# Moving six gathers of a side stream behind the third head of an attention stage, and loading a unit's queries in one transfer

## The chip, the cores and the metric

One core of one Trainium2 chip runs the whole program. The metric is device time in microseconds (us) per execution. The program is written in Tile, where the author gives the order of the work by tracing it, and a planner then places each instruction on its engine's queue by its own estimate of when its operands are ready; an engine then runs its queue strictly in that order.

## The reference

One step of a one-layer decoder over a new prompt of 2048 tokens and over eight running sequences with 8 new tokens each, all in float32:

```python
fq, fk, fv, flogf, mq, mk, mv, ig, lf, og, conv_new = _mixer_inputs(xp, ...)   # one input projection
fox_h = _fox_prompt(fq, fk, fv, flogf)      # 8 heads of 64: causal attention with a forget bias
(C_p, n_p, m_p), m_h = _mlstm_prompt(...)   # 4 heads of 128: matrix memory by chunks
xp = _block_out(xp, fox_h, m_h, ...)        # w_o, layer norm, squared-ReLU MLP 1024-4096-1024, layer norm
k_past = cache_k[l][page_table]             # the sample: 8 sequences with 8192 paged past keys and values
sfox_h = _fox_sample(sq, sk, sv, slogf, k_past, v_past, logf_past)
xs = _block_out(xs, sfox_h, sm_h, ...)
```

## The kernel before

The main line has four stages. Stage A projects the inputs (with the matrix memory beside it). Stage B (`phase_b`) is the prompt's attention. Stage O (`phase_o`) multiplies by `w_o` and norms. Stage C (`phase_c`) is the MLP in four blocks of tokens (`ci` 0 to 3), each with 16 slices of the hidden width (`fc` 0 to 15). Nearly all products are written as three matmuls on float32 split in a high and a low part (`mm3`, lines 157 to 159).

**The stream.** The sample's attention runs beside the main line as a Python generator, `sample_attention`. Each `yield` ends a step. `tick(us)`, which the main line calls with its own estimate of the work just traced, calls `attend()` once per `acc[2]` microseconds, and `attend()` traces the next step; in stages O and C that is every 5 us. A step turns keys, multiplies them (`qk_step`), multiplies values (`pv_step`) and issues the gathers of later pages. `k_gather` (line 1545) is an indirect DMA of 128 rows of 4 KB, 512 KB, issued by POOL into the ring `kT`; `v_gather` (line 1662) does the same for values. `beside` ties every instruction of a step behind the last instruction of the main line on its engine, as far as the dictionary `last` names one.

In stage A the ring has four places. Behind step 78 (`NA + 2`) the stream yields 3, which parks it. The second ring, six places in memory that stage A used, exists from stage B on: the stream then does six gathers of its own with a yield after each of the first five, and goes on with step 79 in the sixth round:

```python
        if n == NA + 2:
            yield 3
            for i in range(6):
                k_gather(NA + i)
                if i < 5:
                    yield 1
```

In stage B `acc[2]` is infinite, so `tick` traces no step there. The loop over units calls `attend()` by hand for units 10 to 15.

At `fc == 13` of block `ci == 2` the main line calls `tick(100.0)` until the stream has ended, and then `sampled()`: the stream's last instructions reduce to `mixs` (line 1706), SP writes that to `dmix` (line 1782), and `sampled` reads `dmix` back as `mxs` (line 1294), splits it into `mhs` and `mls`, and multiplies it by `w_o`.

**Stage B.** 64 units: 8 heads `h`, 8 groups `g` of 256 queries, in that order. `queries(z, g)` (line 970) loads a unit's 64 x 256 queries twice, into partitions 0 to 63 and 64 to 127 of `qn` (three buffers), then ACT splits off `qh` and DVE `ql`. `keys` loads 512 keys of a head, POOL doubles them (`dup`, line 939), PE turns them, ACT and DVE split them into `ks`. `scores(z, g)` works on two tiles of 128 queries: POOL adds the diagonal mask (`nd`, line 990, three buffers), PE multiplies (lines 997 and 998), DVE adds the forget values and takes the maximum (lines 1004 and 1008). `values` of a unit runs one unit later. In head 0 the keys and forget values (`nl`, line 945; `vn`, line 946) come in four parts; those of a later head are loaded during the head before. All of these loads are issued by SP, whose queue also holds the four loads of `w_o` for stage O.

Of the kernel before, what the change touches and what calls it, by code (L numbers as in the profile page):

```python
# [14 lines left out]
OP = mybir.AluOpType  # L15
# [10 lines left out]
S = 2048  # L26
# [21 lines left out]
def dap(ap, off, dims):  # L48
    return bass.AP(tensor=ap.tensor, offset=ap.offset + off, ap=[list(d) for d in dims])
# [3 lines left out]
def body(ctx, tc, I, O, stages):  # L53
    nc = tc.nc
    V, A, G, T, SY = nc.vector, nc.scalar, nc.gpsimd, nc.tensor, nc.sync
# [5 lines left out]
    dq = drm.tile([4, 128, S], F32, name="dq")  # L61
# [39 lines left out]
    acc = [0.0, None, PACE_A, None]  # L101
    macc = [0.0, [], PACE_M]
    last = {}
# [10 lines left out]
    def beside(gen):  # L114

        with ExitStack() as es:
            for i in last.values():
                es.enter_context(tc.issue_after(i.ins))
            return next(gen, 0)

    def attend():

        r = beside(acc[1])
        if r == 3:
            acc[3] = acc[1]
        if r in (0, 3):
            acc[1] = None

    def tick(us):

        macc[0] += us
        while macc[1] and macc[0] > macc[2]:
            macc[0] -= macc[2]
            if beside(macc[1][0]) == 0:
                macc[1].pop(0)
        if not macc[1]:
            macc[0] = 0.0
        acc[0] += us
        while acc[1] is not None and acc[0] > acc[2]:
            acc[0] -= acc[2]  # L140
            attend()
# [6 lines left out]
    def split_hi(dst, src, scale=1.0):  # L148
        last["ACT"] = A.activation(dst, src, AF.Copy, scale=scale)  # L149

    def split_lo(dst, src, hi, eng=None):
        r = (eng or V).tensor_tensor(dst, src, hi.bitcast(F32), op=OP.subtract)  # L152
        if eng is None:
            last["DVE"] = r
# [731 lines left out]
    for bi in range(4):  # L886
        g = block_a(bi)
# [21 lines left out]
    def phase_b():  # L909
# [8 lines left out]
        def bank():  # L918

            turn[0] += 1  # L920
            if turn[0] % 3 == 0:
                return pps.tile([128, 512], F32, name="pS", tag="sX", bufs=1)
            return ppb.tile([128, 512], F32, name="pS", bufs=2)

        def head(h):
            vn = Z[0]["vn"] if h == 0 else pb.tile([128, 16, 64], F32, name="vn", bufs=2)
            nl = pb.tile([128, 2048], F32, name="nl", bufs=2)
            if h == 0:
                masks.append(pb.tile([128, 128], F32, name="dmask"))
            ls = pb.tile([128, 32], F32, name="ls", bufs=2)  # L930
            ks = pb.tile([128, 2048], F32R, name="ks", bufs=2)
            G.memset(ls, 1.0)
            return dict(h=h, ls=ls, nl=nl, vn=vn, ks=ks)
# [8 lines left out]
        def forget_values(z, a, n):  # L942

            h = z["h"]
            SY.dma_start(z["nl"][:, a:a + n], dap(dnl, h * TOT + a, [[0, 128], [1, n]]))
            SY.dma_start(z["vn"][:, a // 128:(a + n) // 128], vp[a:a + n, h * 64:h * 64 + 64].rearrange("(t p) c -> p t c", p=128))
# [4 lines left out]
        def keys(z, g, kn=None):  # L951

            h = z["h"]
            kn = keys_load(h, g) if kn is None else kn
            if h == 0:
                forget_values(z, g * 512, 512)
            pt = ppb.tile([128, 4, 128], F32, name="pt", bufs=3)
            for i in range(4):
                T.transpose(pt[:, i], kn[:, i].rearrange("p d c -> p (d c)"), ident)
            pf = pt.rearrange("p i c -> p (i c)")  # L960
            k = z["ks"][:, g * 512:(g + 1) * 512]
            split_hi(k, pf)
            split_lo(k[64:128], pf[64:128], k[64:128])

        def queries(z, g):

            h = z["h"]
            qn = pb.tile([128, 256], F32, name="qn", bufs=3)
            for d in range(2):
                SY.dma_start(qn[d * 64:d * 64 + 64], dq[h // 2, h % 2 * 64:h % 2 * 64 + 64, g * 256:(g + 1) * 256])  # L970
            qh = pb.tile([128, 256], F32R, name="qh", bufs=3)
            if h == 0 and g == 0:
                z["vn"] = pb.tile([128, 16, 64], F32, name="vn", bufs=2)
            ql = pb.tile([128, 256], F32R, name="ql", bufs=3)
            split_hi(qh, qn)
            split_lo(ql, qn, qh)
            z["q", g] = qh, ql

        def scores(z, g):

            qh, ql = z.pop(("q", g))
            nl, ks = z["nl"], z["ks"]
            out = []
            for i in range(2):
                qt = 2 * g + i
                n = (qt + 1) * 128
                qs = slice(i * 128, i * 128 + 128)
                mx = pb.tile([128, 8], F32, name="mx", bufs=8)
                nd = pb.tile([128, 128], F32, name="nd", bufs=3)
                G.tensor_tensor(nd, nl[:, qt * 128:n], dmask, op=OP.add)  # L990
                st = []
                j = 0
                for a in range(0, n, 512):
                    b = min(n, a + 512)
                    w = max(b - a, 256)
                    pS = bank()
                    T.matmul(pS[:, :w], qh[:, qs], ks[:, a:a + w], start=True, stop=False)
                    last["PE"] = T.matmul(pS[:, :w], ql[:, qs], ks[:, a:a + w], start=False, stop=True)
                    tick(0.42)
                    sp = pb.tile([128, 512], F32, name="S", bufs=10)  # L1000
                    st.append(sp)
                    e = min(b, qt * 128)
                    if e > a:
                        last["DVE"] = V.tensor_tensor_reduce(out=sp[:, :e - a], in0=pS[:, :e - a], in1=nl[:, a:e], scale=1.0, scalar=NEG,
                                               op0=OP.add, op1=OP.max, accum_out=mx[:, j:j + 1])
                        j += 1
                    if b == n:
                        V.tensor_tensor_reduce(out=sp[:, e - a:b - a], in0=pS[:, e - a:b - a], in1=nd, scale=1.0, scalar=NEG,
                                               op0=OP.add, op1=OP.max, accum_out=mx[:, j:j + 1])
                        j += 1  # L1010
                V.tensor_reduce(mx[:, 7:8], mx[:, :j], axis=AX.X, op=OP.max, negate=True)
                out.append((st, mx))
            return out
# [63 lines left out]
        Z = {0: dict(h=0)}  # L1077
        kn = keys_load(0, 0)
        queries(Z[0], 0)
        Z[0].update(head(0))  # L1080
        dmask = masks[0]
# [3 lines left out]
        sc = {}  # L1085
        LA = 1
        for n in range(len(units) + LA):
            if 10 <= n < 16 and acc[1] is not None:
                attend()
            if n == 12:  # L1090
                wo.extend(half_wo(0, q) for q in range(4))
            if n < len(units):
                h, g = units[n]
                sc[n] = scores(Z[h], g)
                if h == 0 and g % 2 == 0 and g < 6:
                    keys(Z[0], g // 2 + 1)
                if h < 7:
                    if g == 3:
                        Z[h + 1] = head(h + 1)
                        forget_values(Z[h + 1], 0, S)  # L1100
                    if g >= 4:
                        keys(Z[h + 1], g - 4)
                if n + 1 < len(units):
                    queries(Z[units[n + 1][0]], units[n + 1][1])
            if n >= LA:
                h, g = units[n - LA]
                values(Z[h], g, sc.pop(n - LA))
# [22 lines left out]
    def half_wo(hf, q):  # L1130

        r = raw().rearrange("p (k c) -> p k c", k=2)
        SY.dma_start(r, I["w_o"][0, q * 256:(q + 1) * 256, hf * 512:(hf + 1) * 512].rearrange("(k p) c -> p k c", p=128))
        return r
# [257 lines left out]
    if "B" in stages:  # L1392
        acc[0], acc[2] = 0.0, PACE_B
        phase_b()
        acc[0], acc[2] = 0.0, PACE_C
# [409 lines left out]
```

## Time and profile before

| | us |
|---|---|
| three runs | 3410.07, 3413.45, 3418.84 |
| median | 3413.45 |
| the profiled execution's own time | 3397.82 |
| its span | 3396.1 |
| PE, DVE, ACT, POOL busy | 3268.6, 2155.7, 1402.1, 896.9 |

Stage B lies at about 950 to 1408 us of the span, stage O at 1408 to 1644, stage C behind it. In the views below a row of a timeline has start, duration, engine, line, operation, tiles, a count, and in brackets how long the engine was idle before it and what ended that. SPq is SP's queue of DMA issues: the duration there is that of issuing. A row of the table by stretches has the stretch, its length, the busy time of PE, PEld, DVE, ACT and POOL with their counts, the granted clock of PE, the mean busy share of the 16 DMA engines, and GB/s.

### The profile page before, as it was taken

What the parts mean: (1) busy time and instruction counts of PE and PEld (TensorE: products, weight loads), DVE (VectorE), ACT (ScalarE), POOL (GpSimd) and SP (SyncE); (2) the same over time, 40 slices, a digit from 0 to 9 for tenths busy, and PEclk for the clock granted to TensorE, in tenths of its full rate; (3) what the DMA queues carried; (4) which work ended last, traced back from release to release, by engine and by line L of the source; (5) the groups of instructions that cost most, each with busy time, mean ns of one, the idle gap of its engine ahead of it and who ended that gap; (6) DMA issues with size and microseconds to landing.
All of it is one profiled execution on the core that took longest, in us unless ns stands there. A gap on an engine that the chain in (4) does not pass through costs nothing. (4 is left out here: it accounts for less than half of the span.)

```text
span 3396.1 us, 59498 instructions
## 1 busy us (share of the span) xinstructions
PE 3268.6 (96%) x22428; PEld 2670.6 (79%) x22428; DVE 2155.7 (63%) x5180; ACT 1402.1 (41%) x2953; POOL 896.9 (26%) x961
## 2 busy tenths in 40 slices
PE   9999999999889999999999999999999999999998
PEld 8998889888866666677777777777777777788887
DVE  5857568556458787655666667666676545644545
ACT  4434235234258888522333233232433333433332
POOL 0121223432322222276432324333233210100001
PEclk9999999999989999999999999999999999999999
DMA  5565675866663232487876758867668654532221
GB/s 170 153 194 164 210 223 178 291 219 211 205 180 90 75 82 59 146 285 252 305 254 228 269 196 301 291 231 256 231 235 316 200 174 144 164 116 87 82 80 66
DMA packets 427240, 646.38 MB, mean 190 GB/s; under 512 B 83148, under 2 KB 320016, under 8 KB 426056
## 3 DMA queue, kind: packets, MB, share of 16 engines
q1 hardware_dynamic: 350184, 363.22, 35.6%
q0 software_dynamic: 74304, 270.57, 21.5%
q10 hardware_dynamic: 2464, 8.78, 0.7%
q8 instruction: 177, 2.90, 0.4%
q14 instruction: 111, 0.91, 0.1%
HBM read 589.63 MB, written 52.83 MB: 189 GB/s over the span
## 5 line engine op out<-in xcount | busy, mean ns | idle before, releaser
L1370 DVE TENSOR_TENSOR y<-y,py 128x512 f32<-128x512 f32 (+1 forms) x475 | 320.3, 680 | 283.7 <-PE py L159 279.4
L149 ACT ACTIVATE wh<-wr 128x1024 fp32r<-128x1024 f32 x268 | 277.9, 1056 | 484.0 <-PE py L159 259.1
L1551 DVE STREAM_TRANSPOSE kT<-kT 128x512 f32<-128x512 f32 x512 | 331.1, 686 | 219.8 <-DMA kT<-cache_k,idxK 219.1
L159 PE MATMUL ph<-x1h,wl 128*128 128x512 f32 (+1 forms) x1280 | 451.4, 354 | 8.3 <-DVE wl L152 8.2
L157 PE MATMUL ph<-x1h,wh 128*128 128x512 f32 (+1 forms) x1280 | 453.4, 354 | 1.9 <-ACT wh L149 1.9
L1545 POOL DMA_INDIRECT kT<-cache_k,idxK x256 | 268.3, 1048 | 700.2 <-PE sQ L1574 639.0
L158 PE MATMUL ph<-x1l,wh 128*128 128x512 f32 (+1 forms) x1280 | 453.2, 354 | 0.0
L157 PE MATMUL py<-wh,hh 128*128 128x512 f32 (+1 forms) x1088 | 430.7, 398 | 4.0 <-DVE y L1368 2.2
L158 PE MATMUL py<-wl,hh 128*128 128x512 f32 (+1 forms) x1088 | 426.0, 392 | 0.0
L159 PE MATMUL py<-wh,hl 128*128 128x512 f32 (+1 forms) x1088 | 425.9, 392 | 0.0
L152 DVE TENSOR_TENSOR wl<-wr,wh 128x1024 fp32r<-128x1024 f32 x268 | 334.4, 1254 | 72.8 <-ACT wh L149 27.1
L157 PE MATMUL pm<-whi,xh 128*128 128x256 f32 (+2 forms) x1088 | 318.5, 293 | 5.9 <-DVE xl L152 3.6
L158 PE MATMUL pm<-wlo,xh 128*128 128x256 f32 (+2 forms) x1088 | 312.5, 287 | 0.8 <-DVE wlo L152 0.8
L159 PE MATMUL pm<-whi,xl 128*128 128x256 f32 (+3 forms) x1088 | 311.2, 286 | 0.0
L159 PEld LDWEIGHTS ph<-x1h,wl 128*128 128x128 f32 x1280 | 240.9, 188 | 43.0 <-DVE wl L152 10.2
L157 PEld LDWEIGHTS ph<-x1h,wh 128*128 128x128 f32 x1280 | 240.9, 188 | 39.8 <-issue 4.1
L158 PEld LDWEIGHTS ph<-x1l,wh 128*128 128x128 f32 x1280 | 241.1, 188 | 36.9 <-issue 4.1
L157 PEld LDWEIGHTS py<-wh,hh 128*128 128x128 f32 (+1 forms) x1088 | 200.8, 185 | 60.8 <-issue 11.9
L159 PEld LDWEIGHTS py<-wh,hl 128*128 128x128 f32 (+1 forms) x1088 | 200.8, 185 | 51.1 <-issue 4.1
L158 PEld LDWEIGHTS py<-wl,hh 128*128 128x128 f32 (+1 forms) x1088 | 201.0, 185 | 39.4 <-issue 0.4
L157 PE MATMUL pm<-xh,whi 128*128 128x256 f32 (+1 forms) x768 | 225.8, 294 | 4.0 <-ACT st L587 3.8
L1662 POOL DMA_INDIRECT vt<-cache_v,idxV x158 | 165.8, 1049 | 219.4 <-PE sO L1686 155.0
(377 smaller groups left out, 6905.2 us busy)
## 6 DMA issues: line engine op xcount, KB each, us to landing
wr<-w SPq DMA_DIRECT2D x256, 512.0 KB
wra<-w_in SPq DMA_DIRECT2D x112, 512.0 KB
Rb<-dR SPq DMA_DIRECT2D x128, 128.0 KB
xn<-x_prompt SPq DMA_DIRECT2D x16, 512.0 KB
qn<-dq SPq DMA_DIRECT2D x128, 64.0 KB
wr<-w_o SPq DMA_DIRECT2D x16, 512.0 KB
xr<-dmix SPq DMA_DIRECT2D x16, 512.0 KB
y<-x_prompt SPq DMA_DIRECT2D x16, 512.0 KB
```

The costliest lines, as they stand in the source:

```text
L149: last["ACT"] = A.activation(dst, src, AF.Copy, scale=scale)
L152: r = (eng or V).tensor_tensor(dst, src, hi.bitcast(F32), op=OP.subtract)
L157: T.matmul(ps, wh, xh, start=first, stop=False)
L158: T.matmul(ps, wh, xl, start=False, stop=False)
L159: last["PE"] = T.matmul(ps, wl, xh, start=False, stop=stop)
L1370: V.tensor_tensor(y, y, ps, op=OP.add)
L1545: G.indirect_dma_start(out=piece(n), out_offset=None, in_=ck, in_offset=IO(ap=idxK[:, b, j // 2, j % 2:j % 2 + 1], axis=0))
L1551: V.transpose(x, x)
L1662: G.indirect_dma_start(out=vt.rearrange("p f c -> p (f c)"), out_offset=None, in_=cv, in_offset=IO(ap=idxV[:, b, (kt % 4) * 4 + kt // 4, f ...
```

## The change

Three edits. The hand-placed `attend()` calls of stage B are gone. POOL's first mask addition of head 2 is entered in `last`, and stays there, so every POOL instruction of the stream traced afterwards is tied behind it. A unit's queries come in one transfer whose source has three dims, 2 x 64 x 256, the first of step 0.

```diff
@@ queries
             qn = pb.tile([128, 256], F32, name="qn", bufs=3)
-            for d in range(2):
-                SY.dma_start(qn[d * 64:d * 64 + 64], dq[h // 2, h % 2 * 64:h % 2 * 64 + 64, g * 256:(g + 1) * 256])
+            SY.dma_start(qn, dap(dq, (h // 2 * 128 + h % 2 * 64) * S + g * 256, [[0, 2], [S, 64], [1, 256]]))
@@ scores
-                G.tensor_tensor(nd, nl[:, qt * 128:n], dmask, op=OP.add)
+                r = G.tensor_tensor(nd, nl[:, qt * 128:n], dmask, op=OP.add)
+                if h == 2 and qt == 0:
+                    last["POOL"] = r
@@ the loop over units
         for n in range(len(units) + LA):
-            if 10 <= n < 16 and acc[1] is not None:
-                attend()
             if n == 12:
```

So the six gathers are now traced by the first six ticks of stage O, and the planner may put them anywhere on POOL's queue behind that mask addition. In the two programs' instruction orders they stand on POOL's queue

```
before: behind head 0's third mask addition
after:  behind head 2's first mask addition, with two more small POOL instructions of the stream (bn, line 1538) right behind them
```

and step 79 of the stream, traced in stage B's unit 15 before, is traced by a tick of stage O after. Counted in matmuls of the main line on PE's queue, all later steps of the stream stand 16 to 223 places further back, most of them near 144; 24 matmuls are one unit of stage O.

## Prediction

> **What bounds the kernel now.** I read the page first, then the table by stretches around the places where the change acts, then the queues in those places.
>
> ```profile
> PE 3268.6 (96%) x22428; PEld 2670.6 (79%) x22428; DVE 2155.7 (63%) x5180; ACT 1402.1 (41%) x2953; POOL 896.9 (26%) x961
> ```
>
> PE is the bound nearly everywhere, so an edit that removes no matmul can act only where PE idles or runs at a low clock. Stage B's start is such a place:
>
> ```profile
> 950.00:960.00 10.00, 3.67 (x20) 2.41 (x18) 4.59 (x20) 2.68 (x8) 3.95 (x10) 0.72 0.65 175
> 960.00:970.00 10.00, 4.32 (x8) 2.45 (x9) 3.74 (x15) 2.68 (x8) 7.82 (x12) 0.50 0.99 291
> 970.00:980.00 10.00, 9.75 (x42) 7.10 (x41) 7.33 (x29) 4.42 (x13) 1.37 (x3) 0.58 0.98 334
> 980.00:990.00 10.00, 7.93 (x53) 5.67 (x52) 6.92 (x26) 7.12 (x20) 2.00 (x5) 1.00 0.90 281
> 990.00:1000.00 10.00, 9.97 (x64) 6.90 (x62) 9.23 (x37) 9.48 (x28) 3.71 (x7) 1.00 0.41 106
> ```
>
> PE is idle 6.3 + 5.7 + 0.3 + 2.1 = 14.4 us of these 50, and its clock is at 0.50 to 0.72 for thirty, while the DMA engines are full from 960 to 980. From 990 on PE is full. What fills the DMA engines, and who is late:
>
> ```profile
> 959.51 1.06 POOL L1545 DMA_INDIRECT kT<-cache_k,idxK  x1 [0.17 <-issue]
> 965.85 0.94 POOL L1545 DMA_INDIRECT kT<-cache_k,idxK  x1 [0.30 <-issue]
> 967.20 0.41 POOL L939 COPY dup<-dup 128x256 f32<-128x256 f32 x1
> 964.86 12.06 SPq L970 DMA_DIRECT2D qn<-dq  x2
> PE pS L997 <- ACT qh L149: 5.4, 2, 3.5
> PE pS L997 <- DVE ks L152: 2.6, 1, 2.6
> ```
>
> The first two rows are the first and the last of six gathers. They hold POOL from 959.5 to 966.8, a copy of keys waits behind them, and SP needs 12 us to issue one unit's two query loads.
>
> **Part 1, the gathers leave the start (gain).** Six gathers of 512 KB are 3.15 MB; at the 291 to 334 GB/s of the rows that is 9.4 to 10.8 us of full DMA engines. If nothing else changed, the loads behind them would land that much earlier and PE would be full about 10 us earlier.
>
> **Part 2, the merged query load (takes most of that back).** Its instruction carries 2 x 64 x 256. The trace has loads with a short leading dim: `qt`, 4 x 32 x 128, two of 64 KB.
>
> ```profile
> 825.05 1.14 SPq L1524 DMA_DIRECT2D qt<-dqb  x2
> 826.50:828.10 1.60, 1.60 (x23) 0.92 (x21) 1.54 (x8) 0.42 (x1) 0.00 (x1) 1.00 0.31 81
> 1130.00:1132.40 2.40, 2.40 (x19) 1.72 (x17) 1.37 (x10) 2.40 (x9) 1.01 (x2) 1.00 0.89 362
> ```
>
> While `qt` moves, the DMA engines are busy by 0.31, five of 16 at most; while a head's `nl` with a leading dim of 128 moves (last row), by 0.89. So I read that a leading dim of 4 keeps to about four engines, and expect two for a leading dim of 2. One busy engine moves 81 / (0.31 x 16) = 16 GB/s by the first row and 362 / (0.89 x 16) = 25 by the second, so 131 kB on two engines take 4.0 to 2.6 us; I take 3.2. Over 16 engines it would be 0.4.
>
> [...]
>
> At the start six such loads (units 1 to 6) follow one another within 30 us: 6 x (3.2 - 0.4) = 17 us more on two of the engines, against 10 us less from the gathers on every engine. [...] Against that, a late query load costs only its unit: unit 4's was issued at 964.86. So the start lies between a gain of 10 and a loss of 17 - 10 = 7. The keys no longer wait for POOL, and the query loads in front of unit 4, which held PE for 5.4 us before, come about as late as they did. I take a gain of 3.
>
> From head 1 on the shortest lead is that of `g = 5`:
>
> ```profile
> 1128.73 0.35 SPq L945 DMA_DIRECT2D nl<-dnl  x1
> 1130.27 6.37 SPq L970 DMA_DIRECT2D qn<-dq  x5
> 1137.47 0.44 ACT L149 ACTIVATE qh<-qn 128x256 fp32r<-128x256 f32 x1
> ```
>
> The load issued at 1130.27 is used at 1137.47. The `nl` ahead of it fills the engines until 1132.4; then 2.6 to 4.0 us give 1135.0 to 1136.4, with about 0.5 to be told of it. It just fits, at about +0.5 over seven heads. SP has 64 fewer issues, which nobody waited for here.
>
> **Part 3, the gathers in head 2 (nothing).**
>
> ```profile
> 1060.00:1065.00 5.00, 5.00 (x35) 3.54 (x33) 4.70 (x17) 4.08 (x13) 0.67 (x2) 1.00 0.01 3
> 1070.00:1075.00 5.00, 5.00 (x37) 3.13 (x36) 4.27 (x17) 4.46 (x12) 0.46 (x1) 1.00 0.01 2
> 1063.29 0.46 POOL L990 TENSOR_TENSOR nd<-nl,dmask 128x128 f32<-128x128 f32 x1 [3.08 <-DVE mx L1008]
> 1070.48 0.46 POOL L990 TENSOR_TENSOR nd<-nl,dmask 128x128 f32<-128x128 f32 x1 [0.93 <-DVE mx L1008]
> 1076.52 0.28 DVE L1008 CUSTOM_DVE_ANT_0 S<-pS,nd 128x128 f32<-128x128 f32 x1
> ```
>
> POOL issues them behind the mask addition of 1063.29 for 6 x 1.25 = 7.5 us, to 1071.3. Behind them are `bn`, a key copy and the next mask addition, which moves from 1070.5 to about 1073 and is needed at 1076.5. The DMA engines are idle there (share 0.01). If that cover went, it would cost 2 us at most.
>
> **Part 4, the stream starts six units later (loss).** Stage O's first six units trace six gathers that are already done, so 144 matmuls pass without stream work. Totals stay, but three places move. At O's start PE had stream matmuls (1.07 us) to do while it waited for weights; they now come where PE is full: +1, between 0 and +2.
>
> ```profile
> 1424.25 1.07 PE L1686 MATMUL sO<-vt,PTs 128*32 128x256 f32 x16
> 1643.35 0.66 PE L1173 MATMUL px<-ident,xr 128*128 128x128 f32 x4 [3.75 <-DVE x1l L152]
> ```
>
> Between O and C, 16 transposes of `x1` stood together and cost a wait of 3.75; after, 24 stand together, two more rounds of ACT and DVE splits: +1.5, between 0 and +4.
>
> The third place is the largest. After the change PE's queue reads (waits in brackets)
>
> ```
> L1693 Matmult sO_29242<-vns_29195,PTn_29189 32x256
> L1702 Matmult sT_30565<-ident_73,os_30563 128x128 [waits DVE_49]
> L157 Matmult py_30585<-wh_30588,mhs_30579 64x256 [waits Activation_49]
> ```
>
> so the stream's last product, its transposes and `sampled`'s first matmul stand next to each other. Before, 72 matmuls of the main line stood between:
>
> ```profile
> 2862.85 0.38 PE L1701 MATMUL sT<-ident,os 128*128 128x128 f32 x2
> 2866.51 0.37 SPq L1782 DMA_DIRECT2D dmix<-mixs  x1
> 2872.79 0.37 SPq L1294 DMA_DIRECT2D mxs<-dmix  x1
> 2878.72 0.63 ACT L149 ACTIVATE mhs<-mxs 128x512 fp32r<-128x512 f32 x1 [7.33 <-PE py L158]
> 2855.80 0.48 DVE L1695 TENSOR_SCALAR os<-sO,rl 128x256 f32<-128x256 f32 x1 [0.88 <-PE sO L1692]
> 2865.61 0.87 DVE L1706 TENSOR_REDUCE mixs<-sT 64x8 f32<-64x16 f32 x8
> 2860.00:2900.00 40.00, 37.63 (x212) 31.93 (x211) 25.88 (x42) 16.75 (x20) 0.56 (x1) 1.00 0.54 168
> ```
>
> Now PE waits for the whole chain: `os` 0.5, `sT` 0.4, `mixs` 0.9, with hand-overs 2.2; the write of `mixs`; the read of `mxs`; `mhs` 0.6. Write and read behind each other stand at the end of stage B:
>
> ```profile
> 1401.54 1.30 SPq L1066 DMA_DIRECT2D drl<-lt  x4
> 1403.78 1.11 SPq L1069 DMA_DIRECT2D rl<-drl  x2
> 1406.99 2.50 POOL L1071 TENSOR_TENSOR ot<-ot,rl 64x512 f32<-64x512 f32 x2 [26.56 <-issue]
> 1420.00:1440.00 20.00, 16.60 (x79) 12.55 (x78) 11.10 (x16) 4.23 (x4) 1.88 (x2) 0.91 1.00 373
> ```
>
> There it took 1403.78 - 1402.5 = 1.3 for the last write and 3.2 for the read, on quiet queues: 4.5, and 7.3 in all. But after the change SP's queue has two loads of `x1` and two of `w_o`, 2.1 MB, right before `mixs`, and the first waits for the same last product. At the 373 GB/s of the last row they take 5.6 us, of which the reductions cover about 1.7: 7.3 + 3.9 = 11.2. PE's clock then falls: in the stretch of the last row an idle 3.4 us left it at 0.91 of 20 us, so 1.8 lost. Against that, PE's 2.4 us of waiting in 2860 to 2900 (weights) should go, since they land during the gap. Sum +10.6, between 7.3 + 1.8 - 2.4 = 6.7 and, if the last value page is late by 3, 13.6.
>
> [...]
>
> **Sum.** -3 + 0.5 + 0 + 1 + 1.5 + 10.6 = +10.6. On the profiled execution (3397.82, its span and 1.7 around it) that is 3408; the median of the runs stands 15.6 above it, so 3424. About 0.3% (10 us) is what a measurement of this kernel can tell from no change.
>
> **Rivals.** (a) The two-engine load decides in every head. It fits at `g = 5` with about 0.6 to 2 us to spare; beyond 5 us it no longer does, and each of heads 1 to 7 pays the excess. At 7 us per load that is 7 x 2 = 14 more: 3438. For it: 1 KB runs and a full `nl` ahead. Against it: no row has an engine as slow as that, 9 GB/s. (b) Not slower: the start is decided by the gathers and not by the query loads. Then keys and forget values arrive 10 us earlier, PE's idle 14.4 us shrink by about 10, and its clock is full earlier, worth 3 more: -13. With the late gap at its low end, 6.7, and the other terms at their low ends, it is -6: 3407; with the last reductions also hidden by matmuls that the trace of before cannot place, -12: 3401. It decides if a query load takes under 1.5 us. For it: POOL and SP, which both stood still because of the gathers, are freed. Against: the four-engine share of `qt`. (c) That the gathers stay where they were: excluded, the new order on POOL shows them in head 2.
>
> **How the numbers follow.** The forecast has 0.60: its own range, -3 to +20 from the terms' ends, has some 0.38 beyond +10 us and 0.22 within. Rival (a) has 0.15, all slower. Rival (b) has 0.25: 0.15 faster by over 10 us, 0.10 within. Faster 0.15, same 0.32, slower 0.53. The time is that of the forecast, 3424; the range reaches from (b)'s end, 3402, to (a), 3438; the forecast's own is 3410 to 3433.
>
> **What would show it.** Right: in the changed profile six gathers near 1060 with PE full around them; a `qn` load that keeps the DMA share near 0.13 for about 3 us; PE full 2 to 4 us earlier than 990; and a wait of some 11 us of PE for `mhs` near 2890, the longest of the profile, with the half clock behind it. Wrong: PE full from 980 or sooner (then (b)), waits of `pS` for `qh` in each head (then (a)), or a gap before `mhs` of under 5 us.

## The result and the profile after

| set | kernel before | changed kernel | ratio, 95% interval |
|---|---|---|---|
| first (6 runs each) | 3411.76 | 3454.49 | 1.0116, 1.0103 to 1.0129 |
| again, in a later set (23 and 6 runs) | 3403.05 | 3428.70 | 1.0079, 1.0058 to 1.0099 |

The changed kernel is slower, by 42.7 us in the first set and by 25.7 in the second. The forecast was +10.6, 3424 in a range of 3402 to 3438; the direction was right, the size was not, and 3454 lies outside the range. All rows "after" below are of the first set's profile (span 3452.8), unless another run is named. Lines from 997 on stand three further down, those from 1089 on one.

**Stage B's start.** The table by stretches of the changed kernel, with its columns as before:

```profile
960.00:970.00 10.00, 3.34 (x13) 2.50 (x13) 2.77 (x13) 2.53 (x8) 2.51 (x6) 0.50 0.64 177
970.00:980.00 10.00, 7.44 (x30) 4.83 (x29) 6.16 (x24) 3.94 (x11) 2.02 (x4) 0.65 0.73 202
980.00:990.00 10.00, 9.66 (x64) 6.72 (x62) 9.08 (x41) 7.71 (x23) 2.53 (x6) 1.00 0.55 144
990.00:1000.00 10.00, 6.12 (x26) 3.95 (x25) 5.80 (x23) 3.91 (x11) 1.34 (x3) 0.70 0.68 224
```

The gathers are gone: the DMA engines are busy by 0.64 and 0.73 where they were full. PE gains nothing by it. It is full from 980 to 990, but then idle for 3.9 us at a stretch, and its clock is at 0.70. Stage B itself began 5.3 us later in this profile (its first key load was issued at 955.99, and at 950.69 in the kernel before). From that load to head 2's first mask addition it takes 114.2 us, and took 112.6. SP's queue and DVE in the timeline show why:

```profile
972.81 6.05 SPq L970 DMA_DIRECT2D qn<-dq  x1
985.53 4.18 SPq L1134 DMA_DIRECT2D wr<-w_o  x4
989.81 0.51 SPq L970 DMA_DIRECT2D qn<-dq  x1
993.47 0.42 DVE L152 TENSOR_TENSOR ql<-qn,qh 128x256 fp32r<-128x256 f32 x1 [2.90 <-ACT qh L149]
```

SP stands for 6.05 us over the issue of one query load, and the loads behind it come later: the one that PE needs near 993 is issued at 989.81 behind four of `w_o`. In the kernel before SP had stood for 12.06 us over two query loads behind the gathers, so what the gathers left free is used up: the query load behind `w_o` is issued 33.8 us after the stage's first key load, and 32.5 us after it in the kernel before. The next two rows are of stretches in which one unit's queries move alone, first in the changed kernel, then in the kernel before:

```profile
1357.00:1360.10 3.10, 3.02 (x20) 2.03 (x19) 2.87 (x14) 3.10 (x11) 1.08 (x2) 1.00 0.12 42
```

```profile
1347.20:1348.50 1.30, 1.30 (x10) 1.15 (x9) 0.80 (x5) 1.30 (x6) 0.17 (x1) 1.00 0.37 101
```

One transfer of 131 kB takes 3.1 us with a share of 0.12, what two engines of 16 give when they are busy throughout (0.125); the two transfers of the kernel before take 1.3 together, with a share of 0.37. The prediction had read two engines from the share of `qt`, and 3.2 us from what one busy engine moved in its rows; this row agrees with both.

**Head 2.** Timeline of POOL, and the stretch:

```profile
1070.87 1.07 POOL L1546 DMA_INDIRECT kT<-cache_k,idxK  x1 [0.27 <-issue]
1077.21 0.94 POOL L1546 DMA_INDIRECT kT<-cache_k,idxK  x1 [0.30 <-issue]
1080.98 0.40 POOL L939 COPY dup<-dup 128x256 f32<-128x256 f32 x1 [2.45 <-DMA dup<-k_prompt]
1081.35 0.45 POOL L990 TENSOR_TENSOR nd<-nl,dmask 128x128 f32<-128x128 f32 x1
```

```profile
1050.00:1100.00 50.00, 47.40 (x331) 32.42 (x330) 37.90 (x149) 39.27 (x110) 17.14 (x29) 1.00 0.41 129
PE pS L1000 <- DVE mx L1011: 2.2, 1, 2.2
```

The first and the last of the six gathers are shown. Behind them stands a key copy that waits 2.45 us for its own load. That load was issued at 1072.29, among the gathers, and the DMA engines are busy by 0.92 from there to 1081. The next mask addition waits behind the copy. (The last row is a line of PE's waits: what it waited for, us in total, how often, the longest.) PE is idle for 50 - 47.40 = 2.6 us in a stretch in which it was idle for 0.1 before.

**The late gap.** Timeline, the stretch around it, and PE's wait:

```profile
2927.65 0.62 PE L1693 MATMUL sO<-vns,PTn 8*32 8x256 f32 x4
2929.41 0.44 PE L1702 MATMUL sT<-ident,os 128*128 128x128 f32 x2 [1.14 <-DVE os L1696]
2930.78 0.37 SPq L1783 DMA_DIRECT2D dmix<-mixs  x1
2935.43 0.37 SPq L1295 DMA_DIRECT2D mxs<-dmix  x1
2938.26 0.63 ACT L149 ACTIVATE mhs<-mxs 128x512 fp32r<-128x512 f32 x1 [10.18 <-DMA mxs<-dmix]
2938.94 0.47 PE L157 MATMUL py<-wh,mhs 128*64 128x256 f32 x1 [9.09 <-ACT mhs L149]
```

```profile
2925.00:2945.00 20.00, 9.77 (x67) 7.92 (x66) 7.62 (x16) 4.53 (x5) 0.00 (x0) 0.74 0.41 129
```

This is the wait that the prediction drew: 1.14 + 9.09 = 10.2 us, the longest of PE's waits in the profile, with the low clock behind it (0.74 over the 20 us of the stretch, 0.50 from 2941 to 2943). The write of `mixs` and its hand-over take 2935.43 - 2930.78 = 4.65 us, the read 2.8.

**An end of a block, which the prediction did not look at.** At the end of the second block PE transposes the next block's tokens, from 2493.7 us on in the kernel before and from 2526.1 in the changed one. The same 45 us in both, from 15 us behind the first of these transposes, by stretch and by DMA queue (q0 is the gathers' queue: packets, MB, share of the 16 engines); the kernel before, and then the changed one:

```profile
2509.00:2554.00 45.00, 44.01 (x248) 34.39 (x248) 31.40 (x52) 20.92 (x29) 24.03 (x18) 1.00 0.69 238
q0 software_dynamic: 808, 2.98, 18.7%
```

```profile
2541.00:2586.00 45.00, 41.95 (x242) 31.33 (x240) 31.55 (x57) 15.07 (x19) 31.46 (x24) 0.96 0.84 295
q0 software_dynamic: 2106, 7.66, 45.3%
```

The gathers move 7.66 MB there instead of 2.98, beside the next block's weights. They are not more, but later: over 76 us from the first transposes both kernels gather about the same, 9.57 MB before (2494 to 2570) and 9.44 after (2526 to 2602). A little later in the changed kernel:

```profile
2590.00:2600.00 10.00, 4.10 (x24) 2.94 (x26) 3.36 (x6) 2.08 (x5) 0.00 (x0) 0.92 0.98 359
2597.53 1.06 ACT L149 ACTIVATE wh<-wr 128x1024 fp32r<-128x1024 f32 x1 [8.64 <-DMA wr<-w]
2599.42 3.21 PE L1575 MATMUL sQ<-kT,qb 128*32 128x256 f32 x27 [5.90 <-ACT PTs L1646]
```

The DMA engines are full (0.98), ACT waits 8.64 us for a weight tile, the stream's copy `PTs` stands behind it on ACT, and PE idles for 5.9 us with a low clock behind (0.74 from 2600 to 2610). The kernel before has no wait of PE over 2.4 us there, and none of ACT for a weight over 3.2 from 2535 us on (one of 8.06 ends at 2508.57, and PE waits for no weight behind it), though its DMA engines are as busy at that place (359 GB/s from 2560 to 2570, the same as in the row above). So it is shown that the tile is late, and that gathers move beside it; that the gathers alone make it late is not shown.

### The profile page after: what moved, and what is told of

Its sections match the earlier page's. It is cut to its first block, busy times and chain, and to the rows that moved or that the text cites. A ratio compares the mean times of both kernels' runs of the same rounds, so it can differ in the third digit from the quotient of the medians.

```text
span 3452.8 us, 59440 instructions
## 1 busy us (share of the span) xinstructions
PE 3298.4 (96%) x22428; PEld 2680.6 (78%) x22428; DVE 2148.3 (62%) x5180; ACT 1401.4 (41%) x2953; POOL 887.5 (26%) x961
## 5 line engine op out<-in xcount | busy, mean ns | idle before, releaser
L1341 ACT ACTIVATE hq<-ph 128x512 f32<-128x512 f32 (+1 forms) x160 | 82.5, 516 | 379.7 <-PE ph L159 311.1
```

The source lines that it names most:

```text
L1341: A.activation(hq, ps, AF.Relu)
```

## The experiments

Theory D: the loss comes from the stream's delay by six units. Rivals: the merged load (L), the gathers' new place (G). The first four kernels ran on one chip, with the kernel before at 3410.11.

**One part of the change at a time.** The merged load alone:

```diff
 (the kernel before)
-            for d in range(2):
-                SY.dma_start(qn[d * 64:d * 64 + 64], dq[...])
+            SY.dma_start(qn, dap(dq, ..., [[0, 2], [S, 64], [1, 256]]))
```

> The kernel before with one edit: a unit's queries in one transfer (2 x 64 x 256). Steps, gathers and the stream stay where they were. Theory D (the loss of the change is the stream's delay by six units of stage O): the load matters only at stage B's start, where SP already stands still behind the gathers, so +0 to +8 us on 3412: 3412 to 3420, and stages O and C as before. Rival L (the two-engine load is what costs): most of the 43 us, 3440 to 3455.

Measured 3423.6: 1.0038 (1.0023 to 1.0053), +13.5 us. Neither theory had it: it is more than D allows, and a third of what L needs. The stretches say where it is:

```profile
970.00:980.00 10.00, 2.11 (x5) 1.15 (x4) 1.48 (x8) 0.42 (x1) 3.43 (x7) 0.50 0.86 291
980.00:990.00 10.00, 8.02 (x30) 6.10 (x31) 5.61 (x25) 4.78 (x13) 1.34 (x4) 0.50 0.68 200
```

With the gathers still at the start and the merged load beside them, PE is almost idle from 960 to 980 (2.19 and 2.11 us busy of 10) and at half clock to 990 (0.50).

The changed kernel with two transfers:

```diff
 (the changed kernel)
-            SY.dma_start(qn, dap(dq, ..., [[0, 2], [S, 64], [1, 256]]))
+            for d in range(2):
+                SY.dma_start(qn[d * 64:d * 64 + 64], dq[...])
```

> The changed kernel with the queries in two transfers again; gathers behind head 2's first mask addition, stream six units late. Theory D: only stage B's start gets better, by 3 to 12 us: 3442 to 3452. Rival L: back to about 3412. At the start, where the profile shows PE full from 980 to 990 on in both kernels, PE should now be full about 8 us earlier than in the changed kernel if the merged load was what held SP there.

Measured 3432.95: 1.0066 (1.0047 to 1.0085), +22.8. That is 9 us below the range that D gave, which was reckoned from the 3454 of the first set; the changed kernel did not run in this one. PE is busy for 8.96 of the 10 us from 970 on and full behind, as (b) of the prediction's rivals had it for a load that does not matter:

```profile
960.00:970.00 10.00, 6.90 (x22) 4.62 (x23) 6.29 (x27) 3.03 (x9) 4.10 (x9) 0.50 0.86 242
970.00:980.00 10.00, 8.96 (x50) 6.29 (x50) 7.74 (x38) 7.15 (x22) 2.27 (x6) 0.92 0.77 213
```

The delay alone:

```diff
 (the kernel before)
-        acc[0], acc[2] = 0.0, PACE_C
+        acc[0], acc[2] = -30.0, PACE_C
```

> The kernel before with one edit: the stream's account starts stage O at -30 us instead of 0, so that its steps come six units later, in the places they have in the changed kernel; gathers in head 0 and two query loads stay. Theory D: the time of the changed kernel less what stage B lost, +30 to +42: 3442 to 3454, with a wait of PE for mhs of 8 to 12 us. Rival G (the gathers' new place in head 2, or the load, is what costs): 3410 to 3418.

Measured 3449.74: 1.0119 (1.0100 to 1.0138), +39.6. Neither the gathers nor the load are touched here, and nearly the whole first result is there: rival G falls as the main cause.

The gathers in head 2 without the delay and without the merged load:

```diff
 (the changed kernel with two transfers)
         for n in range(len(units) + LA):
+            if 17 <= n < 23 and acc[1] is not None:
+                attend()
```

> The changed kernel with two query loads, and with six steps of the stream traced by hand in head 2 (units 17 to 22), behind the mask addition: the gathers lie in head 2, the stream in stages O and C stands exactly where it stood in the kernel before. Theory D: stage B's start gains 8 to 10 us without the gathers, head 2 loses 0 to 4: 3402 to 3412. Rival G: head 2 costs more than the start gains, 3415 to 3425 or above.

Measured 3407.29: 0.9988 (0.9973 to 1.0004), -2.8, no clear difference. On this chip six late units cost 3432.95 - 3407.29 = 25.7 with the gathers in head 2.

**Where the lateness costs.** The next four ran on another chip (the kernel before at 3399.85). Their expectations were written for a kernel before at about 3412, so they are read here as differences to it. The stream ended earlier, so that main-line work stands between it and `sampled`:

```diff
 (the changed kernel)
+                if fc == 13 and ci == 2:
+                    while acc[1] is not None:
+                        tick(100.0)
                 hidden(fc)
...
-                    while acc[1] is not None:
-                        tick(100.0)
                     sampled()
```

> The changed kernel with one edit: the stream is traced to its end before slice 13 of the third block instead of behind it, so that 27 matmuls stand between its last transposes and the first product of sampled. Theory T (the stage's late gap is a price of its own): the wait of PE for mhs falls from 9.1 us to under 2, and 9 to 13 us of the changed kernel's loss go: 3441 to 3446. Rival: the steps pressed into slice 12 cost as much in waits for weights and value pages, and it stays at 3450 or above.

Measured 3419.55: 1.0059 (1.0043 to 1.0075), +19.7. The wait for `mhs` is 1.9 us. Expected were +29 to +34. But that was reckoned from the first set's changed kernel; the repetition below gives the gap's price within one set.

The stream caught up at stage O's first tick:

```diff
 (the changed kernel)
-        acc[0], acc[2] = 0.0, PACE_C
+        acc[0], acc[2] = 30.0, PACE_C
```

> The changed kernel with one edit: the stream's account starts stage O at +30 us, so that six gathers are traced by the first tick and every later step stands where it stood in the kernel before. One query load and the gathers in head 2 stay. Theory S (the parts add): start -8 without the gathers, +10 by the merged load, head 2 +2.5, no late stream: 3411 to 3420. Rival: the merged load delays more than the start (later heads, stages O and C): 3425 to 3435.

Measured 3404.06: 1.0012 (1.0001 to 1.0023), +4.2. Merged load, start without gathers and gathers in head 2 together cost 4; all else is lateness.

Caught up in the first block of stage C, and in the third:

```diff
 (the changed kernel, ci == 0 in the one and ci == 2 in the other)
+                if ci == 0 and 2 <= fc < 8:
+                    acc[0] += 5.0
                 hidden(fc)
```

> The changed kernel with one edit: in slices 2 to 7 of the first block of stage C the stream's account gets 5 us more per slice, so that it is late by six units in stage O only, and stands as in the kernel before from the first block's end on. Theory B (lateness costs at the ends of blocks and at the stream's end, nowhere else): the time of the kernel caught up at stage O within 6 us, 3410 to 3424. Rival E (lateness costs everywhere alike, by the work that is pressed together): 3428 or above.

> The changed kernel with the same edit in the third block instead of the first: the stream is late at both ends of blocks that it passes, and on time at its own end. Theory B: the late gap's 12 us go, the ends of blocks still cost 10 to 20: 3434 to 3445. Rival T2 (the stream's end is all that lateness costs): 3412 to 3424.

Measured 3418.75 (1.0068, 1.0050 to 1.0086) and 3416.91 (1.0052, 1.0039 to 1.0066). They are the same within their intervals, and both stand 13 to 15 above the kernel that is never late in the same set. So theory B as I had put it (late in stage O only costs nothing) is wrong by its time. Rival T2, that the late end is all, falls too: +17.1 where it allowed +12. Rival E expected +16 or above of the first of these two kernels, and its +18.9 fits.

The traces say more of these two. The kernel caught up in the third block is late at the second block's end, and PE has the wait behind `PTs` there, 4.8 us. The kernel caught up in the first block does not have it, but it has another there: 6.5 us for the load of a token tile (`xr`), where the two kernels caught up at stage O wait 1.7 at most. Its steps do not lie quite as in the kernel before, so it does not show that catching up has a price of its own.

**The change again, on one chip with three of these.**

> The changed kernel itself once more, beside the next three and the kernel before on one chip, since the two sets of runs so far had the kernel before at 3410 and at 3400 us, and the same order of work at the ends of blocks cost 26 us in one set and 6 in the other. Theory P (lateness has a price that depends on the chip's run of the transfers in stages O and C): between +25 and +43 over the kernel before, and the same difference to the next two as this set shows it. Rival N (the price is fixed): +43 again, within 5.

> The changed kernel with the stream traced to its end before slice 13 of the third block, again, beside the changed kernel: 9 to 13 us below it (the late gap alone), if the gap is a price of its own. If 20 or more below it, the earlier end also takes waits away elsewhere.

> The changed kernel with the stream caught up at stage O's first tick, again, beside the changed kernel: what lateness costs in all on this chip. Theory P and N both: the kernel before +0 to +10; the changed kernel stands above it by 20 to 40.

> Two query loads, gathers and six steps of the stream in head 2, again: stage B's start without gathers and without the merged load. If the parts add, 6 to 12 us below the kernel caught up at stage O, which differs from it in the merged load alone: the kernel before -8 to 0.

| | us | on the kernel before (3403.05) | ratio, interval |
|---|---|---|---|
| changed | 3428.70 | +25.7 | 1.0079, 1.0058 to 1.0099 |
| changed, early end | 3417.49 | +14.4 | 1.0056, 1.0037 to 1.0075 |
| changed, caught up at O | 3406.82 | +3.8 | 1.0005, 0.9990 to 1.0020 |
| two loads, six steps in head 2 | 3393.01 | -10.0 | 0.9973, 0.9960 to 0.9985 |

By the differences: merged load 13.8; late gap 11.2; the rest of the lateness 10.7; gathers out of the start, with head 2, -10.0. By the spread of the runs each is good to some 4 to 6 us. The last kernel came out below its forecast (-10.0 for -8 to 0). The price of the whole was 42.7 in the first set and is 25.7 here, so rival N falls. The start without gathers and with two transfers, in the last kernel of the table:

```profile
960.00:970.00 10.00, 7.39 (x26) 4.80 (x27) 5.95 (x26) 2.64 (x9) 3.74 (x9) 0.53 0.86 231
970.00:980.00 10.00, 9.28 (x57) 6.21 (x58) 9.24 (x42) 8.64 (x27) 2.74 (x7) 1.00 0.87 228
980.00:990.00 10.00, 9.78 (x63) 6.37 (x57) 9.50 (x37) 8.80 (x26) 2.42 (x6) 1.00 0.80 260
```

PE is at full clock (1.00) from 970 on. The profiles give the start's parts more sharply than the times, from the stage's first key load to head 2's first mask addition: 112.6 us in the kernel before, 123.2 with the merged load alone, 102.5 to 104.5 in the seven kernels with two loads and no gathers there, 113.5 to 115.0 in the eight with the merged load and no gathers. So the gathers' departure is worth 8 to 10 us, and the merged load costs about 11.

Head 2 is covered in the last kernel of the table (the row of 1050 to 1100 in this kernel, and then in the repeated changed kernel):

```profile
1050.00:1100.00 50.00, 49.92 (x350) 34.35 (x346) 39.55 (x161) 42.74 (x122) 19.25 (x31) 1.00 0.46 144
```

```profile
1050.00:1100.00 50.00, 49.64 (x348) 34.56 (x346) 39.95 (x153) 41.80 (x117) 17.30 (x29) 1.00 0.42 135
```

The 2.6 us of the first profile are not in every run of the same code.

**How the price goes with the offset.** Four offsets of the stream in that last kernel, on one chip, with the kernel before at 3400.44:

```diff
 (two loads, six steps in head 2)
-        acc[0], acc[2] = 0.0, PACE_C
+        acc[0], acc[2] = 15.0, PACE_C      # and -10.0, -20.0, -30.0
```

> The kernel with two query loads and its gathers and six steps in head 2, with the stream's account at +15 us at stage O's start: three steps early. Theory G (the price rises with lateness): 0 to 8 us below the kernel with no offset, which was 10 below the kernel before in one set and 3 below in another: the kernel before -3 to -16. Rival F (the price hangs on where the steps fall at the ends of blocks): an offset to either side costs, the kernel before +0 to +10.

> The same kernel at -10 us: two steps late, with 30 matmuls of the main line between the stream's last transposes and the first product of sampled where 72 were, so no late gap yet. Theory G: a third of what six steps cost without the gap, +2 to +5 on the kernel with no offset: the kernel before -7 to 0. Rival F: +6 to +15 on it, the kernel before -2 to +8.

> The same kernel at -20 us: four steps late, no matmul left between the last transposes and sampled, 20 between the last product and sampled. Theory G with the late gap nearly in full: +4 to +8 for lateness and +6 to +9 for the gap, the kernel before +0 to +12. Rival F: as much as at -30 or more, the kernel before +14 or above.

> The same kernel at -30 us: six steps late as in the changed kernel, but with two query loads and the six gathers traced in head 2 by hand. Theory G and F both: +10 to +14 for the gap and +6 to +15 for lateness, the kernel before +8 to +22; on a chip like that of the first sets up to +30. If it stands under +5, the delay was not the cause of the changed kernel's loss.

| offset | us | ratio, interval |
|---|---|---|
| 3 steps early | 3401.31 | 1.0001, 0.9988 to 1.0014 |
| 2 late | 3391.71 | 0.9972, 0.9960 to 0.9984 |
| 4 late | 3417.11 | 1.0045, 1.0026 to 1.0065 |
| 6 late | 3410.76 | 1.0039, 1.0024 to 1.0055 |

The price does not rise step by step: two steps late costs nothing (the kernel with no offset stood at 0.9973 in the set before), three early stand 9.6 us above two late, four late cost as much as six. Theory G falls: it missed three of its four ranges. F held at three steps early, four late and six late, and missed at two late, where it expected -2 or more on the kernel before. The jump of 25.4 us between two and four is only in part the late gap. PE's longest waits in the stages O and C at four late, and then those around the stream's end at six late:

```profile
PE py L157 <- ACT mhs L149: 8.2, 1, 8.2
PE sT L1646 <- ACT PTs L1648: 6.5, 1, 6.5
```

```profile
PE py L157 <- ACT mhs L149: 9.5, 1, 9.5
PE sT L1704 <- DVE os L1698: 1.1, 1, 1.1
```

At two late, 30 matmuls of the main line stand behind the last transposes, and there is no wait for `mhs`. What else is in the jump was not settled; the 6.5 us for `PTs` are a single wait that the kernel two steps late does not have. Two of these kernels beat both kernels of the case: two loads with six steps in head 2 (0.9973, though 0.9988 and not clear in the other set), and the same two steps late (0.9972).

## Why the prediction was wrong

**The late gap: right, its size partly by luck.** +10.6 was forecast, by 11.2 us for the chain; the chain took 10.2 in the profile, and taking it away was worth 11.2 (3428.70 - 3417.49). The loads queued on SP ahead of `mixs` did not add the 3.9 taken for them: the write was issued 2930.78 - 2929.41 = 1.4 us after the transposes began. The write itself was longer instead, 4.65 where 1.3 was taken. The two errors nearly cancel.

**The merged load: engines and duration right, price wrong.** Two engines (a share of 0.12) and 3.2 us (3.1) were right. That the leading dim sets the number of engines was the author's reading of two shares, 0.31 at 4 and 0.89 at 128; the 0.12 at 2 fits it, and no run varied the dim alone. Nor does a run show that the two engines held up the other loads, which the 7 of loss at the start takes for granted; what the runs show is SP standing for 6.05 us over the issue of one such load. The failed step is the sentence that a late query load costs only its unit. All loads stand in one order on SP, and with the merged load the whole order came later: the query load behind `w_o` was issued 33.8 us after the first key load, and 27.1 us after it with two loads and no gathers. SP's longest single stop is not the difference: with two loads it stood still at the same place too, for 5.38 us. The merged load costs 13.5 to 13.8, near the 17 that the prediction worked out as the sum of the six loads; its -3 left only 7 for it. The gathers' departure was worth 8 to 10 at the start, as forecast (10); with head 2 it gained 2.8 and 10.0 in two sets where the load did not stand against it. Start and head 2 together were +4 in two sets, not -3.

**Head 2: nearly right.** Nothing was forecast, and 2 at most if the cover went. The cover named was POOL's; what went was another, the DMA engines under a key load. 2.6 us in one profile, 0.4 in another.

**Later heads: right.** No price per head; from 1200 to 1300 of the changed profile:

```profile
1200.00:1300.00 100.00, 99.92 (x701) 69.03 (x699) 80.28 (x308) 83.85 (x233) 25.82 (x43) 1.00 0.27 74
```

So rival (a), 3438 by seven heads of 2 us, came nearest to the time, for a reason that this row rules out.

**From O to C: no change.** +1.5 was forecast for eight more transposes together. They waited twice, 2.1 + 1.5 = 3.6 us, and once for 3.75 before:

```profile
PE px L1174 <- DVE x1l L152: 2.1, 1, 2.1
PE px L1174 <- DVE ln L167: 1.5, 1, 1.5
```

**The step that failed most: "Totals stay, but three places move".** Six late steps cost 21.9 us on one chip (3428.70 - 3406.82) and 25.7 on another, of which the gap is 11; the term for the rest was 1 + 1.5. I followed the stream to its end and never asked what else its steps meet on the way. A stream that moves by six units also meets the ends of the blocks at another of its steps. At the second block's end its gathers then come later, beside the next block's weights, and PE waits (5.9 us in the first profile) and drops to half clock (0.50 from 2600 to 2604). The repeated changed kernel has the same wait:

```profile
PE sQ L1575 <- ACT PTs L1646: 3.9, 1, 3.9
```

It is in each of the eight profiles in which the stream is six steps late there, with 3.9 to 6.0 us, and in none of the six in which it is on time from stage O on. So this place is shown for about half of the 10.7 us. Where the other half lies is not shown.

In the second set the shortfall adds up: 25.7 - 10.6 = 15.1 is 8.8 of lateness (21.9 for 1 + 1.5 + 10.6 = 13.1) and 6.3 of start and later heads (+3.8 for -3 + 0.5).

**What stays open.** The first set had 17 us more of loss than the later set, for the same kernel. In the two profiles the main line is 2.3 us apart at the end of stage B (9.5 and 7.2 us behind the kernel before) and 29 us apart (45 and 16) behind the second block's end, so the difference arises in stages O and C. From 1410 to 2990 us PE's waits sum to 63.6 us in the first profile and 47.1 in the repeated one; 8.2 of the first are spent on nothing that the profile shows, and none of the second. What those are, and what makes the rest, was not settled. And the delay alone on the kernel before (39.6) is dearer than the same delay with the gathers in head 2 (25.7) on the same chip. Its profile has one wait that the other late ones lack, 8.9 us at the first block's end for the sums `y`; why it arises there alone was not settled either.

## What to carry to other kernels

Price work that runs beside a main line not only by the room that it needs but also by the places that it meets: here the same work six steps later cost 21.9 and 25.7 us. When an edit shifts a whole stream, go along it from end to end: at its end look for a chain that now stands alone (here 10 us), and at each peak of the main line's transfers see which of the stream's transfers fall there before and after. Count them over a longer stretch as well, to tell more bytes from later bytes.

Of a transfer, read from a lone one how many engines carry it before merging two into one (here a share of 0.12 for 3.1 us, where the two had 0.37 for 1.3); and where one queue issues all loads, price a slow load by everything behind it in the queue, not by its own consumer (here 13.5 to 13.8 us where 7 was allowed).

## What was not expected of the hardware

One load of 131 kB held SP's issue for 6.05 us, and for 6.09 in the profile of the merged load alone, twice the 3.1 us that such a load takes to move. Two plain loads at the same place held it for 5.38 us without the gathers, and for 12.06 behind them.

The same kernel differs between sets, by more than an edit is worth: the kernel with two loads and six steps in head 2 took 3407.29 and 3393.01 us in two sets, the changed kernel 3454.49 and 3428.70, while the kernel before took 3411.76 to 3399.85 in the five sets. Differences were therefore taken within a set.
